# Block products for three quarters of an MLP down-projection, with weight sums on GpSimd

## The chip, the core and the metric

The kernel runs on one core of a Trainium2 chip. A core has five engines that run side by side, each through its own list of instructions in order: TensorE (PE; its weight loads are listed as PEld), VectorE (DVE), ScalarE (ACT), GpSimd (POOL) and SyncE (SP), which here only issues DMAs. They wait for each other by semaphores. The metric is the device time of one execution in microseconds (us); the median of several runs is compared.

## What is computed

The reference is one decoder block on 512 tokens of width 1024 in float32. Two token mixers (a state-space scan and a gated delta rule) are merged by gates and projected; then comes a squared-ReLU MLP. Each of the two parts has a norm ahead and one behind:

```python
x = x + g1 * rmsnorm(merged @ w_out, norm_mix_post)
h = rmsnorm(x, norm_mlp_pre) * (1.0 + sc2) + sh2
y = jnp.square(jax.nn.relu(h @ w_mlp_up)) @ w_mlp_down      # 1024 -> 4096 -> 1024
x = x + g2 * rmsnorm(y, norm_mlp_post)
```

The change concerns the last product, `... @ w_mlp_down`, and what stands between `merged @ w_out` and it.

## The kernel before

**Matmuls.** Every float32 operand is split into two float32r parts, hi and lo. ACT makes hi by a cast, DVE makes lo by subtracting hi from the raw value (`dense_w`, L140 to L147: `raw` by a DMA on SP, `sc.copy` at L145, `ve.tensor_sub` at L146). `mm3` (L149 to L152) then issues three matmuls for each pair of tiles: hi x hi, lo x hi, hi x lo. `raw`, `whi` and `wlo` have three buffers each.

**Order of work.** The first 870 us (projections in, scans) are ordered by a planner written into the kernel (`Weave`) and are not touched, apart from four small tables and `eye`, which the change allocates in another pool. Behind it, from the up-projection of the two mixers on, the order within each engine is made by the framework when the kernel is built: it goes through an estimate of time and places an instruction on its engine when its inputs and its buffers are free there, the one written earlier first. So an instruction can stand in its engine's list far ahead of its place in the program. On the chip each engine takes its list in that order. A pool's memory that is given to a later pool can be used only after the earlier pool's last reader.

**From the output projection to the MLP** (L1268 to L1356). The pool `yp` of the up-projection is closed (L1268), and `lp` is opened. The rows for the two gates are loaded (`adr`, then a bias row added and a norm row multiplied in on DVE, L1275 to L1279), as are the four residual tiles `x1` (L1284). The output projection goes by halves of the tokens (`half`) and halves of the columns (`hf`), with four weight tiles `kp` each (L1333 to L1348). `sums` squares on ACT; `norms(half)` (L1303 to L1325) takes the root on POOL (L1308), scales on DVE (L1313), adds the residual, one half of the columns on POOL and one on DVE (L1318), squares again on ACT (L1322), takes the second root on POOL (L1324) and scales into `xn` (L1325). `chans(half)` transposes `xn` on TensorE (L192) and makes the split `h2`. `up_part` computes the first three hidden tiles for one half of the tokens, so that TensorE has something to do while the second half is normed.

**The MLP** (L1359 to L1438) goes by quarters `q` of the 4096 hidden channels. In a quarter, eight hidden tiles (128 channels x 512 tokens, 24 matmuls of 128x512 each) are made, squared and split into `act` (L1375 to L1379). Then `down` (L1382) goes over two halves of the output columns `hf` and four weight tiles `kp`; in each, four token tiles x two channel tiles x three matmuls of 128x512. The four banks are copied to `ya` in the first quarter and added to it on DVE (L1410) in the others. The last quarter ends with the norm and the output.

PSUM has eight banks; `lpsum` hands them out in turn.

## Time and profile before

| | |
|---|---|
| median of 3 runs | 1483.22 us (1481.3 to 1486.84) |
| the profiled execution, its own time | 1484.77 us |
| its span (first to last instruction) | 1483.1 us, granted clock 0.996 |
| TensorE busy, weight loads busy | 1458.1 us (98%), 1241.0 us (84%) |
| DVE, ACT, POOL busy | 862.5 us (58%), 732.6 us (49%), 370.2 us (25%) |
| matmuls | 8592 |
| HBM | 181.1 MB read, 16.88 MB written, 133 GB/s over the span |

Busy matmuls overlap, since each record holds the passage through the array; the distance from one start to the next tells more than a record's length. In a table of stretches each engine has its busy time in the stretch and, in brackets, its number of instructions; then come the granted clock, the share of time in which the DMA engines were busy, and their rate. A group of instructions has its line, engine, operation and tiles, its count, its busy time and the mean of one in ns, and behind the bar the idle time of the engine ahead of it with what ended it.

### The profile page before, as it was taken

To read this page: it belongs to the slowest core of one execution; us is meant where nothing else is said; L and a number is where in the kernel's file an instruction comes from. 1 tells how busy PE (TensorE), PEld (TensorE's weight loads), DVE (VectorE), ACT (ScalarE), POOL (GpSimd) and SP (SyncE) were. 2 spreads that over 40 slices of the span, in tenths; PEclk is the share of its full clock that TensorE was granted. 3 is DMA by queue.
4 is the path that set the end of the run, shared out by engine and by line. 5 is a ranking of instruction groups with operands and counts; after the bars stand their busy time and mean duration, and the time that the engine had idled before them with its cause. 6 is when DMAs were issued, how large, how long until landed. Compare 5 with 4: busy or idle time off the path is not lost. (4 is left out here: it accounts for less than half of the span.)

```text
span 1483.1 us, 22692 instructions
## 1 busy us (share of the span) xinstructions
PE 1458.1 (98%) x8592; PEld 1241.0 (84%) x8592; DVE 862.5 (58%) x1522; ACT 732.6 (49%) x1379; POOL 370.2 (25%) x691
## 2 busy tenths in 40 slices
PE   9999999999999999999999899999999999999998
PEld 7788898879989889888888788888878888888886
DVE  3565577677767777676777634444477324343444
ACT  6575545673764747645665635333355333132232
POOL 3005444341814607336623410000011000000002
PEclk9999999999999999999999999999999999999999
DMA  9323434543434524344343449543372233223221
GB/s 360 127 97 118 150 103 125 128 137 97 151 119 138 158 81 151 121 116 138 116 137 119 158 170 331 175 156 127 110 239 88 97 100 100 89 96 99 93 95 69
DMA packets 87070, 199.47 MB, mean 134 GB/s; under 512 B 32504, under 2 KB 33024, under 8 KB 86960
## 3 DMA queue, kind: packets, MB, share of 16 engines
q1 hardware_dynamic: 86960, 198.01, 41.3%
q8 instruction: 68, 1.11, 0.3%
q14 instruction: 42, 0.34, 0.1%
HBM read 181.10 MB, written 16.88 MB: 133 GB/s over the span
## 5 line engine op out<-in xcount | busy, mean ns | idle before, releaser
L150 PE MATMUL ps<-hT,whi 128*128 128x512 f32 x688 | 285.7, 415 | 4.8 <-ACT whi L469 4.3
L151 PE MATMUL ps<-hT,wlo 128*128 128x512 f32 x688 | 269.8, 392 | 1.2 <-DVE wlo L471 1.2
L152 PE MATMUL ps<-hT,whi 128*128 128x512 f32 x688 | 269.9, 392 | 0.0
L146 DVE TENSOR_TENSOR wlo<-raw,whi 128x1024 fp32r<-128x1024 f32 x114 | 140.0, 1229 | 199.7 <-ACT whi L145 199.7
L145 ACT CAST whi<-raw 128x1024 fp32r<-128x1024 f32 x114 | 119.4, 1048 | 210.1 <-PE pl L151 61.9
L150 PE MATMUL ps<-whi,hT 128*128 128x256 f32 (+1 forms) x536 | 166.3, 310 | 2.2 <-ACT y L715 1.4
L471 DVE TENSOR_TENSOR wlo<-raw,whi 128x1024 fp32r<-128x1024 f32 x103 | 128.1, 1244 | 64.2 <-ACT whi L469 60.3
L150 PEld LDWEIGHTS ps<-hT,whi 128*128 128x128 f32 x688 | 129.9, 189 | 31.9 <-ACT whi L469 4.5
L152 PE MATMUL ps<-wlo,hT 128*128 128x256 f32 (+1 forms) x536 | 154.3, 288 | 0.6 <-DVE wlo L471 0.6
L151 PE MATMUL ps<-whi,hT 128*128 128x256 f32 (+1 forms) x536 | 153.8, 287 | 0.0
L152 PEld LDWEIGHTS ps<-hT,whi 128*128 128x128 f32 x688 | 129.7, 189 | 28.3
L151 PEld LDWEIGHTS ps<-hT,wlo 128*128 128x128 f32 x688 | 130.1, 189 | 25.8 <-DVE wlo L471 2.4
L469 ACT CAST whi<-raw 128x1024 fp32r<-128x1024 f32 x103 | 107.3, 1044 | 67.4 <-PE ps L152 47.1
L533 DVE SCALAR_TENSOR_TENSOR cv<-ps,col,cv 128x511 f32<-128x511 f32 (+1 forms) x180 | 133.0, 742 | 8.0 <-ACT cv L527 5.4
L150 PEld LDWEIGHTS ps<-whi,hT 128*128 128x128 f32 x536 | 102.1, 190 | 5.8 <-ACT y L715 1.6
L825 POOL TENSOR_TENSOR tm<-Ub,Nb 128x60 f32<-128x60 f32 (+24 forms) x248 | 93.7, 378 | 52.5 <-DMA Nb<-btd 37.6
L151 PEld LDWEIGHTS ps<-whi,hT 128*128 128x128 f32 x536 | 102.1, 190 | 2.2
L152 PEld LDWEIGHTS ps<-wlo,hT 128*128 128x128 f32 x536 | 101.8, 190 | 2.0 <-DVE wlo L471 0.8
L827 POOL TENSOR_TENSOR Ub<-Ub,tm 128x60 f32<-128x60 f32 (+24 forms) x248 | 95.0, 383 | 19.4
L1416 POOL TENSOR_TENSOR ya<-ya,gate 128x512 f32<-128x512 f32 x4 | 5.8, 1466 | 324.8 <-ACT junk L1414 324.8
L150 PE MATMUL pl<-hT,whi 128*128 128x512 f32 (+1 forms) x184 | 66.6, 363 | 1.0 <-DVE hT L195 1.0
L151 PE MATMUL pl<-hT,wlo 128*128 128x512 f32 (+1 forms) x184 | 66.1, 362 | 0.4 <-DVE wlo L146 0.4
(502 smaller groups left out, 3049.0 us busy)
## 6 DMA issues: line engine op xcount, KB each, us to landing
raw<-in_w_ch SPq DMA_DIRECT2D x81, 512.0 KB
raw<-in_w_ada SPq DMA_DIRECT2D x48, 512.0 KB
raw<-in_w_z SPq DMA_DIRECT2D x32, 512.0 KB
raw<-in_w_up SPq DMA_DIRECT2D x32, 512.0 KB
raw<-in_w_mu SPq DMA_DIRECT2D x32, 512.0 KB
raw<-in_w_md SPq DMA_DIRECT2D x32, 512.0 KB
dc<-acd SPq DMA_DIRECT2D x16, 512.0 KB
ydr<-y SPq DMA_DIRECT2D x32, 256.0 KB
```

Source lines behind the costliest of these rows:

```text
L145: sc.copy(hi, raw)
L146: ve.tensor_sub(out=lo, in0=raw, in1=hi.bitcast(F32))
L150: pe.matmul(ps, lhsT=lhs[0], rhs=rhs[0], start=first, stop=False)
L151: pe.matmul(ps, lhsT=lhs[1], rhs=rhs[0], start=False, stop=False)
L152: pe.matmul(ps, lhsT=lhs[0], rhs=rhs[1], start=False, stop=last)
L469: sc.copy(hi, raw)
L471: ve.tensor_sub(out=lo, in0=raw, in1=hi.bitcast(F32))
L533: ve.scalar_tensor_tensor(out=t[:, s:], in0=ps[:, :T - s], scalar=col[:, o + k:o + k + 1], in1=t[:, s:], op0=MUL, op1=ADD)
L825: gp.tensor_tensor(out=t3, in0=Ub[:, 0:r, j:j + 1].to_broadcast([P, r, n]), in1=Nb[:, j:j + 1, j + 1:32].to_broadcast([P, r, n]), op=MUL)
L827: gp.tensor_tensor(out=Ub[:, 0:r, j + 1:32], in0=Ub[:, 0:r, j + 1:32], in1=t3, op=SUB)
L1416: gp.tensor_tensor(out=y, in0=y, in1=gates[1][:, hs], op=MUL)
```

## The change

**Seven products instead of eight.** Two hidden tiles (k = 0, 1) and two halves of the tokens make four blocks of the squared activations, a0 to a3 (`a[:, 2k + half]`, 256 tokens each); two hidden tiles and two halves of the output columns make four blocks of weights (`b[hf][:, k]`). The plain product takes eight block products. The change uses a known form with seven, with sums of blocks as factors: on the activations a0, a2; the two sums in `s12`; a0 - a1 and a3; a2 less a sum; on the weights `b[0]`, the two sums in `t`, the two differences that are written back into `b`, and one more in `b[1][:, 1]`. It does so in the first three quarters (`down7`), in four stages of two, two, two and one product, each over four weight tiles `kp`, two token tiles and the three matmuls of a split product. Some products are added to two outputs: their bank is read, and matmuls go on adding to it in the next stage (`pa`, `pb_`). A quarter so has 14 additions to `ya`.

**Who does it.** The sums of weights and of activations are made on POOL. The splits are made on ACT and DVE as before, but from the sums, on the activations for each of the first three stages (`unit`), with the subtraction of the fourth on POOL; `ahead` makes those of stages three and four some steps early. The first quarter's weights are loaded by DMAs that POOL issues, and their sums made, beside the output projection's first half; the other quarters' are loaded by SP.

**What moves.** The rows of the gates and the residual tiles are loaded on POOL's queue from within the output projection (`residual`), into a pool that is open only until the MLP. So `x1` is stored to DRAM after each norm (`x1d`) and loaded again for the last quarter. The last quarter keeps its code.

```diff
-    tok1 = const.tile([P, NC, P], F32, name="tok1")
+    tok1 = sp.tile([P, NC, P], F32, name="tok1", bufs=1)
...
-    lp = ctx.enter_context(tc.tile_pool(name="lp", bufs=1))
-    gates = []
-    for n in range(2):
-        g = fin.tile([P, D], F32, name=f"gate{n}")
-        nc.sync.dma_start(out=g, in_=adr[n].partition_broadcast(P))
-        for r, fn in ((n, ve.tensor_add), (2 + n, ve.tensor_mul)):
-            bb = lp.tile([P, D], F32, tag="ob", name="rb", bufs=2)
-            nc.sync.dma_start(out=bb, in_=rows[r].partition_broadcast(P))
-            fn(out=g, in0=g, in1=bb)
-        gates.append(g)
+    x1d = dram.tile([NC, P, D], F32, name="x1d")
+    gate1 = fin.tile([P, D], F32, name="gate1")
+    rp = ctx.enter_context(tc.tile_pool(name="rp", bufs=1))
+
+    def quarter_weights(q, kp, en):
+        b = []
+        for hf in range(2):
+            b.append(rp.tile([P, 2, T], F32, tag="wr", name="wr", bufs=8))
+            en.dma_start(out=b[hf].rearrange("p a b -> p (a b)"), in_=w_md[q, hf, kp])
+        t = rp.tile([P, 2, T], F32, tag="tt", name="tt", bufs=4)
+        gp.tensor_tensor(out=t[:, 0], in0=b[1][:, 0], in1=b[0][:, 0], op=SUB)
+        gp.tensor_tensor(out=t[:, 1], in0=b[1][:, 1], in1=t[:, 0], op=SUB)
+        gp.tensor_tensor(out=b[1][:, 0], in0=b[1][:, 1], in1=b[1][:, 0], op=SUB)
+        return b[0], b[1], t
...
+    def residual():
+        for n, g in enumerate((gate0, gate1)):
+            gp.dma_start(out=g, in_=adr[n].partition_broadcast(P))
+            for r, fn in ((n, ve.tensor_add), (2 + n, ve.tensor_mul)):
+                bb = lp.tile([P, D], F32, tag="ob", name="rb", bufs=2)
+                gp.dma_start(out=bb, in_=rows[r].partition_broadcast(P))
+                fn(out=g, in0=g, in1=bb)
+        for t in range(NC):
+            xx = lp.tile([P, D], F32, name=f"x1{t}")
+            gp.dma_start(out=xx, in_=x[t * P:(t + 1) * P, :])
+            x1.append(xx)
...
+            nc.sync.dma_start(out=x1d[t], in_=x1[t])
...
                 if half and hf and kp == 2:
                     chans(0)
+                if not half and not hf and kp == 2:
+                    residual()
+                if not half and hf:
+                    first_q.append(quarter_weights(0, kp, gp))
...
+    def halves(src, dst, en):
+        sc.copy(dst[0], src)
+        en.tensor_tensor(out=dst[1], in0=src, in1=dst[0].bitcast(F32), op=SUB)
+        return dst
+
+    def unit(src, n, en):
+        u = mp.tile([P, 2, n, 256], F32R, tag="act", name="unit", bufs=8)
+        return halves(src, (u[:, 0], u[:, 1]), en)
+
+    def wide(src, en=None):
+        n = src.shape[1]
+        return halves(src, [wp.tile([P, 2, T], F32R, tag=tag, name=tag)[:, 0:n] for tag in ("whi", "wlo")], en or ve)
+
+    def product(ps, u, ub, w, wb, tt, first, last):
+        ts = slice(tt * P, (tt + 1) * P)
+        for n, (i, j) in enumerate(((0, 0), (1, 0), (0, 1))):
+            pe.matmul(ps, lhsT=u[i][:, ub, ts], rhs=w[j][:, wb], start=first and n == 0, stop=last and n == 2,
+                      skip_group_check=True)
+
+    def down7(q):
+        ab, pr, u1, u2 = [], [], [], []
+        for kp in range(4):
+            ab.append(first_q[kp] if q == 0 else quarter_weights(q, kp, nc.sync))
+            a = mp.tile([P, 4, 256], F32, tag="pr", name="pr", bufs=4)
+            for k in range(2):
+                _, rl = hidden(q * 8 + 2 * kp + k)
+                sc.activation(a[:, 2 * k:2 * k + 2].rearrange("p a b -> p (a b)"), rl, AF.Square)
+            pr.append(a)
+            sm = mp.tile([P, 2, 256], F32, tag="s12", name="s12", bufs=4)
+            gp.tensor_tensor(out=sm[:, 0], in0=a[:, 1], in1=a[:, 3], op=ADD)
+            gp.tensor_tensor(out=sm[:, 1], in0=sm[:, 0], in1=a[:, 0], op=SUB)
+            gp.tensor_tensor(out=a[:, 1], in0=a[:, 0], in1=a[:, 1], op=SUB)
+            u1.append(unit(a[:, 0:4:2], 2, ve))
+            gp.tensor_tensor(out=a[:, 2], in0=a[:, 2], in1=sm[:, 1], op=SUB)
+            if kp:
+                u2.append(unit(s12, 2, ve))
+            s12 = sm
+        u2.append(unit(s12, 2, ve))
...
+        def ahead():
+            n = step[0]
+            step[0] += 1
+            if 3 <= n < 7:
+                u3.append(unit(pr[n - 3][:, 1:4:2], 2, ve))
+            elif 7 <= n < 11:
+                u4.append(unit(pr[n - 7][:, 2:3], 1, gp))
+
+        def stage(us, ws, plan, read=None):
+            for kp in range(4):
+                ahead()
+                w = ws(kp)
+                for n, (ps, ub, wb, start) in enumerate(plan if kp < 3 else plan[::-1]):
+                    for tt in range(2):
+                        product(ps[tt], us[kp], ub, w, wb, tt, start and kp == 0, kp == 3)
+                        if kp == 3 and n == 0 and read:
+                            read(tt)
...
+        def w1(kp):
+            b1, _, t = ab[kp]
+            w = wide(b1)
+            gp.tensor_tensor(out=b1[:, 1], in0=b1[:, 1], in1=t[:, 1], op=SUB)
+            return w
+
+        def w3(kp):
+            w = [wp.tile([P, 2, T], F32R, tag=tag, name=tag) for tag in ("whi", "wlo")]
+            for n in range(2):
+                halves(ab[kp][n][:, 1 - n], (w[0][:, n], w[1][:, n]), ve)
+            return w
+        stage(u1, w1, [(pc, 1, 1, True), (pa, 0, 0, True)], lambda tt: add(tt, 0, pa[tt], True))
+        for tt in range(2):
+            add(tt, 0, pc[tt])
+        pb_ = banks()
+        stage(u2, lambda kp: wide(ab[kp][2]), [(pb_, 0, 0, True), (pa, 1, 1, False)],
+              lambda tt: add(tt, 1, pa[tt], True))
+        for tt in range(2):
+            add(tt + 2, 1, pb_[tt], True)
+        pc = banks()
+
+        def third(tt):
+            add(tt + 2, 1, pa[tt])
+            add(tt + 2, 0, pa[tt], True)
+        stage(u3, w3, [(pc, 1, 0, True), (pa, 0, 1, False)], third)
+        for tt in range(2):
+            add(tt + 2, 0, pc[tt])
+        stage(u4, lambda kp: wide(ab[kp][1][:, 1:2]), [(pb_, 0, 0, False)])
+        for tt in range(2):
+            add(tt, 1, pb_[tt])
+
+    for q in range(3):
+        down7(q)
...
+    x1 = [rp.tile([P, D], F32, tag="tt", name="x1r", bufs=4) for _ in range(NC)]
+    for t in range(NC):
+        nc.sync.dma_start(out=x1[t], in_=x1d[t])
```

`add` copies a bank to `ya` on ACT (the first time in quarter 0) or adds it there on DVE.

More of the change, by code (lines that the diff above doesn't have):

```diff
@@ L401, in hybrid_block @@
     H = 48
-    tok1 = const.tile([P, NC, P], F32, name="tok1")
-    tok2 = const.tile([P, NC, P], F32, name="tok2")
-    neg = const.tile([P, NC, 16], F32, name="neg")
-    elast = const.tile([P, H, NC], F32, name="elast")
+    tok1 = sp.tile([P, NC, P], F32, name="tok1", bufs=1)
+    tok2 = sp.tile([P, NC, P], F32, name="tok2", bufs=1)
+    neg = sp.tile([P, NC, 16], F32, name="neg", bufs=1)
+    elast = sp.tile([P, H, NC], F32, name="elast", bufs=1)
     nA = const.tile([H, 1], F32, name="nA")
@@ L415, in hybrid_block @@
         gp.memset(tl, 0.0)
-    eye = const.tile([P, 8, 32], F32, name="eye")
+    eye = sp.tile([P, 8, 32], F32, name="eye", bufs=1)
     gp.memset(eye, 0.0)
@@ L1268, in hybrid_block @@
     up.close()
-    lp = ctx.enter_context(tc.tile_pool(name="lp", bufs=1))
-    gates = []
-    for n in range(2):
-        g = fin.tile([P, D], F32, name=f"gate{n}")
-        nc.sync.dma_start(out=g, in_=adr[n].partition_broadcast(P))
-        for r, fn in ((n, ve.tensor_add), (2 + n, ve.tensor_mul)):
-            bb = lp.tile([P, D], F32, tag="ob", name="rb", bufs=2)
-            nc.sync.dma_start(out=bb, in_=rows[r].partition_broadcast(P))
-            fn(out=g, in0=g, in1=bb)
-        gates.append(g)
-    x1, xn = [], []
-    for t in range(NC):
-        xx = fin.tile([P, D], F32, name=f"x1{t}")
-        nc.sync.dma_start(out=xx, in_=x[t * P:(t + 1) * P, :])
-        x1.append(xx)
+    x1d = dram.tile([NC, P, D], F32, name="x1d")
[11 more added lines that the diff above has]
+        return b[0], b[1], t
+    norm_scope = ExitStack()
+    lp = norm_scope.enter_context(tc.tile_pool(name="lp", bufs=1))
+    gate0 = lp.tile([P, D], F32, name="gate0")
+    x1, xn = [], []
+    def residual():
[9 more added lines that the diff above has]
+            x1.append(xx)
     h2 = [(chan_tile(), chan_tile()) for _ in range(KD)]
@@ L1309, in norms @@
         for t in tt:
-            xx = lp.tile([P, D], F32, tag="act", name="xn", bufs=16)
+            xx = lp.tile([P, D], F32, tag="xn", name="xn", bufs=4)
             for i in range(2):
@@ L1330, in chans @@
             to_channels(lp, lpsum, None, 1, xn, (h2[kt][0][:, cs], h2[kt][1][:, cs]), kt, (2 * half, 2 * half + 1))
-    pp = {}
+    pp, first_q = {}, []
     for half in range(2):
@@ new lines, in hybrid_block, with hidden @@
+    norm_scope.close()
+    mp = ctx.enter_context(tc.tile_pool(name="mp", bufs=1))
+    ya = [mp.tile([P, D], F32, name=f"ya{t}") for t in range(NC)]
+    sq = [mp.tile([P, 1], F32, name=f"sqn{t}") for t in range(NC)]
+    def hidden(mm):
+        if mm < len(ups):
+            ps = ups[mm][1]
+        else:
+            w = dense_w(w_mu[mm])
+            ps = lpsum()
+            for k in range(KD):
+                ks = slice(k * P, (k + 1) * P)
+                mm3(ps, (w[0][:, ks], w[1][:, ks]), h2[k], k == 0, k == KD - 1)
+        rl = mp.tile([P, T], F32, tag="rl", name="rl", bufs=2)
+        sc.activation(rl, ps, AF.Relu)
+        return ps, rl
@@ new lines, in down7, with add @@
+    def down7(q):
[17 more added lines that the diff above has]
+        u2.append(unit(s12, 2, ve))
+        def add(tt, hf, ps, first=False):
+            y = ya[tt][:, hf * T:(hf + 1) * T]
+            if first and q == 0:
+                sc.copy(y, ps)
+            else:
+                ve.tensor_add(out=y, in0=ps, in1=y)
+        u3, u4, step = [], [], [0]
+        def ahead():
[14 more added lines that the diff above has]
+                            read(tt)
+        banks = lambda: [lpsum() for _ in range(2)]
+        pa, pc = banks(), banks()
+        def w1(kp):
[26 more added lines that the diff above has]
+            add(tt, 1, pb_[tt])
@@ new lines, in hybrid_block, with down @@
+    for q in range(3):
+        down7(q)
+    act = []
+    for m in range(8):
+        ps, rl = hidden(24 + m)
+        a = mp.tile([P, 2, T], F32R, tag="act", name="act", bufs=8)
+        s = mp.tile([P, T], F32, tag="pr", name="sq", bufs=4)
+        ve.scalar_tensor_tensor(out=s, in0=ps, scalar=0.0, in1=rl, op0=MAX, op1=MUL)
+        sc.activation(a[:, 0, :], rl, AF.Square)
+        ve.tensor_sub(out=a[:, 1, :], in0=s, in1=a[:, 0, :].bitcast(F32))
+        act.append(a)
+    def down(ps, t, w, kp, a=0, b=T):
+        ts = slice(t * P, (t + 1) * P)
+        for k in range(2):
+            kk = 2 * kp + k
+            mm3(ps[:, a:b], (act[kk][:, 0, ts], act[kk][:, 1, ts]),
+                (w[0][:, k * T + a:k * T + b], w[1][:, k * T + a:k * T + b]), kk == 0, kk == 7)
```

120 lines of the change are left out of this document (43 added, 77 removed).

## The prediction

> **What bounds the kernel now.** I read the page first, then the stretches of the last 410 us, then single rows.
>
> ```profile
> span 1483.1 us, 22692 instructions
> PE 1458.1 (98%) x8592; PEld 1241.0 (84%) x8592; DVE 862.5 (58%) x1522; ACT 732.6 (49%) x1379; POOL 370.2 (25%) x691
> ...
> PEclk9999999999999999999999999999999999999999
> ...
> PE 40%; DVE 2%; DMA 1%; issue 0%; ACT 0%; POOL 0%; POOLq 0%; SPq 0%; DVEq 0%; ACTq 0%
> ```
>
> TensorE is busy 98% of the span at full granted clock, and the chain of waits hardly names anything else, so the time is the number of matmuls times their spacing, plus the few places where TensorE starves.
>
> The table of stretches, one line each (us, then busy time and instruction count by engine, clock, DMA share, GB/s):
>
> ```profile
> 1074.00:1094.00 20.00, 20.00 (x90) 16.53 (x89) 13.45 (x13) 10.15 (x16) 0.00 (x0) 1.00 0.82 277
> 1094.00:1116.00 22.00, 20.45 (x97) 16.34 (x96) 16.87 (x26) 13.01 (x22) 5.72 (x5) 1.00 0.63 203
> 1116.00:1134.00 18.00, 15.61 (x117) 13.86 (x116) 14.72 (x37) 9.23 (x18) 5.91 (x5) 1.00 0.10 33
> 1211.00:1255.00 44.00, 44.00 (x196) 36.40 (x195) 18.86 (x22) 16.14 (x24) 0.00 (x0) 1.00 0.30 96
> 1255.00:1299.00 44.00, 44.00 (x191) 35.69 (x190) 15.76 (x17) 9.25 (x10) 0.00 (x0) 1.00 0.29 96
> ```
>
> The last two are one MLP quarter: up (22 DVE instructions) and down (17). TensorE has no gap, DVE and ACT are under half busy and POOL, where the change puts much of its work, does nothing. The first three are output projection and norms; there TensorE loses 1.55 + 2.39 us, and the DMA share reaches 0.82.
>
> **What is removed: 72 matmuls.** A down quarter issues 2 halves x 4 weight tiles x 4 token tiles x 2 x 3 = 192 matmuls of 128x512. Its spacing comes from where the phases begin:
>
> ```profile
> 1211.11 0.39 PE L150 MATMUL pl<-hT,whi 128*128 128x512 f32 x1
> ...
> 1254.64 0.40 PE L150 MATMUL pl<-whi,act 128*128 128x512 f32 x1
> ...
> 1299.27 0.39 PE L150 MATMUL pl<-hT,whi 128*128 128x512 f32 x1
> ```
>
> Up takes 43.53 us / 192 = 0.2267 us each, down 44.63 / 192 = 0.2324. A quarter by block products has 7 products of 4 tiles x 2 token tiles x 3 = 168 matmuls of the same shape. Three quarters save 72 x 0.2324 = **16.7 us**. If the products ran at the spacing of up, it would be 3 x (44.63 - 168 x 0.2267) = 19.6 us; the stationary operand stays an activation slice as in down, so I take 16.7.
>
> **What is added on ACT and DVE, per quarter.**
>
> ```profile
> L146 DVE TENSOR_TENSOR wlo<-raw,whi 128x1024 fp32r<-128x1024 f32 x80 | 98.3, 1231 | 118.1 <-ACT whi L145 118.1
> L145 ACT CAST whi<-raw 128x1024 fp32r<-128x1024 f32 x80 | 83.7, 1046 | 138.8 <-PE pl L151 61.9 <-PE ps L151 49.9 <-PE ps L152 15.7
> L1379 DVE TENSOR_TENSOR act<-sq,act 128x512 fp32r<-128x512 f32 x32 | 21.9, 685 | 0.0
> L1378 ACT ACTIVATE act<-rl 128x512 fp32r<-128x512 f32 x32 | 20.1, 629 | 0.0
> L1410 DVE TENSOR_TENSOR ya<-pl,ya 128x512 f32<-128x512 f32 x14 | 9.5, 688 | 3.1 <-PE pl L152 2.8
> ```
>
> DVE after: 16 splits of 1024 columns (8 up, 8 in the first two stages) x 1.23 = 19.7; 24 splits of 512 (12 activation sums, 8 weights of stage three, 4 of stage four) x 0.685 = 16.4; 14 additions instead of 8 x 0.688 = 9.6: 45.7 us where the two windows show 34.6. ACT: 16 x 1.05, 24 casts and 8 squares at 0.63, 8 Relu of much the same: about 43 us. A quarter on TensorE becomes 43.5 + 39.0 = 82.5 us, so both have room on average.
>
> The narrow place is the product stages: 39.0 us of TensorE against 9.8 + 5.5 + 2.7 (weights) + 2.7 (third stage's activation sums) + 9.6 (additions) = 30.3 us of DVE. Weights have three buffers, so a split may start two steps (2 x 2.79 us) ahead. At the seams a bank is read and written again: the bank closes 6 matmuls before the stage ends and is next used after 6 more, 12 x 0.2324 = 2.8 us; two additions of 0.69 need 1.4 plus latency. That is hidden unless DVE is more than about 1.2 us behind. The last stage has steps of 1.39 us, and in its 5.6 us DVE has six additions, two splits and the next up split, 4.1 + 1.4 + 1.2 = 6.7 us, some 1 us over. No row shows such a seam: at best 0, at worst 1 us at each of 3 seams in 3 quarters, 9. I take 0.8 us a quarter, **+2.5**, nearer to nothing because this kernel's own bank seams (L1410) show no matmul waiting for them.
>
> **What is added on POOL.** Each quarter 16 subtractions of 512 columns and 20 operations of 256. Their nearest rows (shortest/median/longest ns):
>
> ```profile
> L1416 POOL TENSOR_TENSOR ya<-ya,gate x4: 1289/1380/1812, 1451.4 to 1456.8; 128x512 f32<-128x512 f32 x4
> ...
> L1156 POOL TENSOR_TENSOR xk<-xk,zs x32: 733/744/1721, 228.1 to 870.7; 128x256 f32<-128x256 f32 x32
> ...
> L471 DVE TENSOR_TENSOR wlo<-raw,whi x103: 1209/1226/1759, 56.1 to 857.8; 128x1024 fp32r<-128x1024 f32 x103
> ```
>
> 16 x 1.29 + 20 x 0.74 = 35.4 us alone, of 82.5. Per up pair (10.9 us) it is 3 x 1.29 + 4 x 0.74 = 6.8 us, so POOL keeps up, and what it makes is needed a stage later (11 us). But both engines now and then take most of another's instruction longer: 744 becomes 1721, 1226 becomes 1759. That is one waiting out the other.
>
> The Trainium skill, "SBUF — State Buffer", section "Who interferes with whom", says why: a DVE instruction with two SBUF inputs and a GpSimd instruction that reads SBUF share a port, and the second blocks until the first is done. This trace agrees (1721 against 744 ns). By the rule nearly all splits here contend with the new POOL work; it is the slower rival below.
>
> **What is moved.** Now SP loads gate and residual rows early, and only the bias and norm rows late:
>
> ```profile
> 911.39 0.90 SPq L1275 DMA_DIRECT2D gate<-adr  x2
> ...
> 914.73 1.35 SPq L1284 DMA_DIRECT2D x<-in_x  x2
> ...
> 1073.88 0.80 SPq L1278 DMA_DIRECT2D rb<-in_rows  x2
> ```
>
> ```profile
> 1073.12 0.69 DVE L1266 TENSOR_TENSOR hT<-ma,hT 128x512 fp32r<-128x512 f32 x1
> ```
>
> L1278 goes out 0.07 us after the last reader of the up-projection's pool. Gate 0 and the residual move into that later space, so with the first quarter's weights 17 of 18 DMAs of 512 KB now start there, all on POOL's queue, gate 1's `adr` row alone being free earlier. Bandwidth: 277 GB/s at share 0.82 makes about 340 GB/s when full (estimate). From 1074 to 1116 the rows above carry 20 x 277 + 22 x 203 = 10.0 MB, of which 2 MB are the rows; 18 x 0.52 = 9.4 MB plus two stores of x1 make 18.4 MB, 54 us at 340. So the loads run to about 1128, the weights last. For the issue, SP takes 0.4 us each (0.80 for 2); POOL's nearest is one operation, 1.29: 7 to 23 us for 18, ending at 1081 to 1097, and the residual's ten of them by 1087 at the latest, ahead of the first use of gate 0 (1094.91, below).
>
> The Trainium skill, "DMA: Bandwidth & Descriptors", section "Latency and other measured facts", puts the first byte of a GpSimd-issued DMA at about 1 us, spent on emitting it; as an estimate that is 18 us for 18, between the bounds. No run here shows it yet.
>
> What stands behind them on POOL is the norm chain:
>
> ```profile
> 1116.92 0.70 POOL L1308 TENSOR_TENSOR r<-r,mhalf 128x2 f32<-128x2 f32 x1 [13.38 <-DVE r L1307]
> 1118.48 2.96 POOL L1318 TENSOR_TENSOR x<-xn,x 128x512 f32<-128x512 f32 x2 [0.86 <-DVE xn L1313]
> 1124.13 1.73 POOL L1324 TENSOR_TENSOR s<-s,mhalf 128x1 f32<-128x1 f32 x1 [2.69 <-DVE s L1323]
> 1126.86 0.55 POOL L1324 TENSOR_TENSOR s<-s,mhalf 128x1 f32<-128x1 f32 x1 [1.00 <-DVE s L1323]
> ```
>
> ```profile
> 1094.91 2.07 DVE L1313 SCALAR_TENSOR_TENSOR xn<-pl,r,gate 128x512 f32<-128x512 f32 x3 [1.04 <-POOL r L1308]
> ...
> 1127.44 0.75 DVE L1325 TENSOR_SCALAR xn<-x,s 128x1024 f32<-128x1024 f32 x1 [0.73 <-POOL s L1324]
> ```
>
> ```profile
> 1128.26 0.60 PE L192 MATMUL pl<-ident,xn 128*128 128x128 f32 x4
> ```
>
> The second half's `xn` is ready at 1128.19 (the last root ends at 1127.41, L1325 follows), and TensorE starts on it 0.07 us later. So delay of a POOL step there goes to the end one for one. Three times in turn (root, residual addition, root) the chain comes back to POOL, which may then be in a weight sum: nothing if the sums are done by 1117, all twelve (12 x 1.47 = 17.6) if they stand ahead. Against it, the removal of SP's rows from among the weight loads may give back the one long wait there, 1.2 us on L146. By the bandwidth the sums of the last one or two weight tiles come after 1117, so I take one sum of 1.3 at each of three returns: **+4** (from -1 to +18). SP also gets four stores of x1, which wait for that chain with the next up weights behind them; three raw buffers cover some 3 x 5.4 us.
>
> Past the three quarters nothing changes on the path: the last one and the output are as before, and reloading x1 (four DMAs) lies under the last quarter's 192 up matmuls. The small tables that change pools change address only.
>
> **Sum.** -16.7 + 2.5 + 4 = -10.2. Span 1483.1 becomes 1472.9; the profiled execution lasted 1484.77, 1.67 around its span, so 1474.6 for one like it. It was 1.55 above the median of 1483.22, which makes the forecast **1473.0**.
>
> **Rivals.** (1) All cover holds: seams and norms cost nothing, 1483.2 - 16.7 = 1466.5. For it speaks that DVE and ACT are half idle; against it that TensorE waits already at the second norm.
> (2) POOL's queue holds the norms: ten or more sums or loads ahead of the root of the second half, +14 to 17.6 with 2.5 of seams: about 1484, no change. For it speaks the 54 us of loads into 42; against it that the sums come in pairs of tiles as they land, with room for the root between.
> (3) Slower: the port. In the stages DVE has 39.0 - 30.3 = 8.7 us free. POOL has 4 x 1.29 + 4 x 0.74 = 8.1 there, and the next quarter's 12 sums (15.5) if they come early. If DVE waits out all, 53.9 us in 39.0: 14.9 lost in each of two quarters (the third has no next sums), 1483.2 - 16.7 + 29.8 + 4 = 1500. It decides once more than 8.7 us of a quarter's stages is lost to POOL. Against it: the sums need buffers which the fourth stage frees, so they fall into the up phase.
> (4) The products do not run at the spacing assumed, since the last stage's 1.39 us steps wait for splits: 0.5 us x 12 steps more, 1479.
>
> **Chances.** Forecast 0.54 (its own range 1468 to 1478), (1) 0.18, (2) 0.17, (3) 0.07, (4) 0.04. A measurement can tell 0.5%, 7.4 us: below 1475.8 is faster, above 1490.6 slower. Faster: (1) and four fifths of the forecast, 0.61; slower: (3), 0.07; the rest, 0.32. The range leaves out half of (1), at the low end, the dear end of (2), and (3): 1466 to 1484.
>
> **What would show it.** TensorE with 8520 matmuls; quarters of 82 to 84 us instead of 88.2 (1211.11 to 1299.27); in them no wait over 1 us at a split or an addition; POOL with some 106 to 125 us more; the stretch from the last output-projection matmul to the first full up matmul longer by 1 to 7 us with a POOL root or sum behind it. Wrong would be: gaps inside the stages of several us (then 3 or 4), or an unchanged norm stage (then 1).

## The result and the profile after

The changed kernel is slower: 1495.34 us, median of 4 runs (1494.33 to 1497.62), against 1484.08 us for 4 runs of the kernel before; ratio 1.0078, 95% interval 1.0055 to 1.0101. The forecast was 1473.0 us, faster. The page of the profile after, its span, its engines, the clock and the queue that POOL issues:

```profile
span 1493.2 us, 22889 instructions
...
PE 1447.0 (97%) x8520; PEld 1228.5 (82%) x8520; DVE 929.9 (62%) x1570; ACT 777.2 (52%) x1463; POOL 517.5 (35%) x817
...
PEclk9999999999999999999999999999997999999999
...
q0 software_dynamic: 2592, 9.44, 1.8%
```

The 72 matmuls are gone and TensorE's busy time fell by 11.1 us, yet the span grew by 10.1. The stretches of the norm stage and of the second quarter (hidden tiles, then products), in the columns used before:

```profile
1074.00:1094.00 20.00, 17.23 (x75) 13.54 (x74) 9.54 (x8) 7.17 (x12) 6.78 (x13) 1.00 0.93 329
1094.00:1116.00 22.00, 19.04 (x82) 14.78 (x81) 13.20 (x10) 7.90 (x9) 13.23 (x11) 1.00 0.94 348
1116.00:1134.00 18.00, 3.78 (x17) 2.63 (x16) 9.56 (x13) 5.38 (x11) 12.18 (x11) 0.67 0.48 170
1134.00:1150.00 16.00, 14.88 (x94) 13.03 (x94) 12.14 (x29) 7.96 (x18) 4.91 (x5) 0.84 0.34 133
...
1227.21:1270.79 43.58, 43.58 (x193) 36.02 (x192) 20.12 (x17) 18.40 (x27) 22.71 (x19) 1.00 0.32 104
1270.79:1311.95 41.16, 39.79 (x169) 31.34 (x168) 38.21 (x40) 21.40 (x34) 23.39 (x18) 1.00 0.28 89
```

From 1116 to 1134 TensorE has 17 instructions where it had 117. The DMA share is 0.93 and 0.94 in the two stretches ahead, where it was 0.82 and 0.63. In the quarter, DVE is busy 38.21 of 41.16 us of the products; the forecast had counted 30.3 of 39.0.

Set out by stages, each from the start of its first matmul to the start of the next stage's, in us. "Norm stage" runs from the first output-projection matmul to the first product (down matmul before) of the first quarter, "last" from the first hidden tile of the last quarter to the end:

| kernel | norm stage | products 1 | hidden 2 | products 2 | hidden 3 | products 3 | last | span |
|---|---|---|---|---|---|---|---|---|
| before | 98.31 | 44.64 | 43.53 | 44.63 | 43.54 | 44.63 | 95.6 | 1483.1 |
| after | 119.36 | 40.19 | 43.58 | 41.16 | 43.89 | 41.09 | 96.3 | 1493.2 |

The norm stage lost 21.05 us. The three quarters gained 4.45 + 3.42 + 3.19 = 11.06, and the last stage lost 0.7.

Where the 21 us appear, by the timelines of the kernel after. TensorE:

```profile
1093.13 0.50 PE L152 MATMUL pl<-wlo,hT 128*128 128x512 f32 x1 [2.45 <-DVE wlo L146]
...
1132.45 1.09 PE L192 MATMUL pl<-ident,xn 128*128 128x128 f32 x4 [13.87 <-issue]
```

DVE, the step ahead of the first half's root:

```profile
1098.82 0.17 DVE L1324 TENSOR_SCALAR r<-r 128x2 f32<-128x2 f32 x1
```

POOL, on which that root (L1325) stands:

```profile
1102.16 1.48 POOL L1282 TENSOR_TENSOR tt<-wr 128x512 f32<-128x512 f32 x1 [10.71 <-DMA wr<-in_w_md]
...
1117.45 1.29 POOL L1284 TENSOR_TENSOR wr<-wr 128x512 f32<-128x512 f32 x1
1118.69 0.71 POOL L1325 TENSOR_TENSOR r<-r,mhalf 128x2 f32<-128x2 f32 x1
1121.80 1.42 POOL L1282 TENSOR_TENSOR tt<-wr 128x512 f32<-128x512 f32 x1 [2.40 <-DMA wr<-in_w_md]
...
1127.06 2.50 POOL L1335 TENSOR_TENSOR x<-xn,x 128x512 f32<-128x512 f32 x2
```

The root's input is ready at 1098.99; the root runs at 1118.69, behind nine weight sums and the waits for their loads (POOL stood still for 10.71 us waiting for the first). Three more sums stand between the root and the residual addition (L1335). TensorE waits 13.87 us ahead of the transposes of the first half; the profile names no releaser there ("issue"), but the transposes read `xn`, which that chain makes.

### The profile page after: what moved, and what is told of

It reads as the page before. It is cut to its first block, busy times and chain, and to the rows that moved or that the text cites. A ratio compares the mean times of both kernels' runs of the same rounds, so it can differ in the third digit from the quotient of the medians.

```text
span 1493.2 us, 22889 instructions
## 1 busy us (share of the span) xinstructions
PE 1447.0 (97%) x8520; PEld 1228.5 (82%) x8520; DVE 929.9 (62%) x1570; ACT 777.2 (52%) x1463; POOL 517.5 (35%) x817
## 5 line engine op out<-in xcount | busy, mean ns | idle before, releaser
L146 DVE TENSOR_TENSOR wlo<-raw,whi 128x1024 fp32r<-128x1024 f32 x90 | 119.4, 1328 | 152.9 <-ACT whi L145 152.8
L471 DVE TENSOR_TENSOR wlo<-raw,whi 128x1024 fp32r<-128x1024 f32 x103 | 128.9, 1253 | 63.1 <-ACT whi L469 61.7
L145 ACT CAST whi<-raw 128x1024 fp32r<-128x1024 f32 x90 | 94.3, 1048 | 127.8 <-PE pl L152 42.3
L469 ACT CAST whi<-raw 128x1024 fp32r<-128x1024 f32 x103 | 107.3, 1044 | 69.2 <-PE ps L152 48.5
L1418 PE MATMUL pl<-whi,unit 128*128 128x512 f32 x240 | 75.5, 396 | 1.0 <-DVE ya L1448 1.0
L1402 DVE TENSOR_TENSOR wlo<-wr,whi 128x512 fp32r<-128x512 f32 (+1 forms) x48 | 51.2, 1090 | 38.3 <-ACT whi L1401 33.9
```

The lines of the kernel that those rows point to most:

```text
L145: sc.copy(hi, raw)
L146: ve.tensor_sub(out=lo, in0=raw, in1=hi.bitcast(F32))
L469: sc.copy(hi, raw)
L471: ve.tensor_sub(out=lo, in0=raw, in1=hi.bitcast(F32))
L1402: en.tensor_tensor(out=dst[1], in0=src, in1=dst[0].bitcast(F32), op=SUB)
L1418: pe.matmul(ps, lhsT=u[i][:, ub, ts], rhs=w[j][:, wb], start=first and n == 0, stop=last and n == 2, skip_group_check=True)
```

## The experiments

Stages in all of them are read as above; the numbers are gathered in one table at the end. The first six split the norm stage and the last five the quarters. Where the text gives no ratio, the kernel ran once, and its stages and span are those of that one execution.

**Without the first quarter's sums.** Only the 12 sums go; the loads stay where they are. The first quarter then multiplies unsummed weights.

```diff
-                    first_q.append(quarter_weights(0, kp, gp))
+                    first_q.append(quarter_weights(0, kp, gp, False))   # loads, no sums
```

> The changed kernel with the 12 sums of the first quarter's weights on POOL left out (the first quarter then uses unsummed weights; all 18 loads stay on POOL's queue). In the changed kernel the first half's root L1325 runs at 1118.7, 20 us after its input, and TensorE idles 13.9 us. Theory A (POOL's list: the root stands behind sums that wait for their loads): the root runs within 2 us of its input, the idle stretch of 13.9 us shrinks to under 3 us, span 1476 to 1481. Rival B (DMA bandwidth: 18 loads make the gate, the residual and the output projection's weights late): the idle stretch stays above 8 us and the span above 1486.

The wait ahead of the transposes fell to 1.4 us (from 13.87), and the norm stage to 108.24 us: 11.1 us of the 21 are the sums. The span, 1483.3 us, was above the 1476 to 1481 expected, since 9.9 us of the norm stage remained.

**The sums moved, nothing left out.** The loads stay on POOL's queue; the 12 sums are placed behind the second half's last `hT` (the tiles that `chans` makes from the transposed `xn`).

```diff
+    mark = gp.tensor_tensor(out=flag, in0=lo, in1=lo, op=ADD)      # lo: last column of the last hT
+    with tc.issue_after(mark.ins):
+        first_q = [quarter_sums(b) for b in first_q]
```

> The changed kernel with one thing moved and nothing left out: the first quarter's 12 weight sums stand on POOL behind the last hT of the second half (by a 128x1 operation that reads that tile), instead of beside the output projection. All loads stay where the change has them, on POOL's queue. Theory A (the place of the sums on POOL's list alone made 11 of the 21 us of the norm stage; the rest is the early loads and the rows): the first half's root runs within 1 us of its input, TensorE's wait ahead of the transposes falls from 13.9 to under 2 us, norm stage 106 to 109 us, first quarter's products 40 to 42, span 1480 to 1485. Rival B (the loads keep POOL or DVE as late as the sums did): wait over 8 us, norm stage over 114.

The norm stage took 108.22 us, as without the sums (108.24), the wait ahead of the transposes was 1.58 us, and the first products took 41.73. The root ran at 1098.15 with its input ready at 1097.83. So it is the place on POOL's list that cost 11 us, not the work. The span was 1485.7, just over the range expected.

**First quarter's weights late.** Their loads and sums go where those of the other quarters are; the rows and the residual stay on POOL's queue.

```diff
-                    first_q.append(quarter_weights(0, kp, gp))
...
-            ab.append(first_q[kp] if q == 0 else quarter_weights(q, kp, nc.sync))
+            ab.append(quarter_weights(q, kp, nc.sync))
```

> The changed kernel with the first quarter treated as the second and third: its weights loaded on SP and summed within the quarter, the pool for them opened behind the norms. The ten row and residual loads stay on POOL's queue. Both theories: norm stage shorter. A: the root runs within 2 us of its input, the time from the start of the output projection to the first product falls from 119.4 us to 103 to 107 (99 before the change gave 98.3), the first quarter's products take about 41 us like the other two; span 1477 to 1482, ratio to before 0.995 to 1.0. B: the same stretch 100 us, since only ten of 18 loads are left.

Norm stage 105.22, as expected, but products 46.40 in place of 41: ratio 1.0041 (1.0025 to 1.0057), where faster was expected. So 3.0 us more of the norm stage belong to the early loads, and 7.1 us above the 98.1 of the kernel that undoes both remain. DVE's timeline of this kernel shows them:

```profile
1082.26 1.23 DVE L1297 TENSOR_TENSOR gate<-gate,rb 128x1024 f32<-128x1024 f32 x1 [3.90 <-DMA rb<-in_rows]
1083.41 1.22 DVE L146 TENSOR_TENSOR wlo<-raw,whi 128x1024 fp32r<-128x1024 f32 x1
...
1090.72 1.23 DVE L1297 TENSOR_TENSOR gate<-gate,rb 128x1024 f32<-128x1024 f32 x1 [3.54 <-DMA rb<-in_rows]
1091.86 1.22 DVE L146 TENSOR_TENSOR wlo<-raw,whi 128x1024 fp32r<-128x1024 f32 x1
...
1095.30 1.22 DVE L1297 TENSOR_TENSOR gate<-gate,rb 128x1024 f32<-128x1024 f32 x1 [2.23 <-DMA rb<-in_rows]
```

and TensorE's what follows from it:

```profile
1093.13 0.50 PE L152 MATMUL pl<-wlo,hT 128*128 128x512 f32 x1 [2.70 <-DVE wlo L146]
1097.72 0.50 PE L152 MATMUL pl<-wlo,hT 128*128 128x512 f32 x1 [1.57 <-DVE wlo L146]
1104.88 0.50 PE L152 MATMUL pl<-wlo,hT 128*128 128x512 f32 x1 [1.43 <-DVE wlo L146]
```

The gate's operations wait on DVE for their rows, and the splits of the output projection's weights stand behind them. TensorE loses 5.7 us to it. The first of these operations ran at 1082.26; in the kernel before it ran at 1078.85. POOL's list adds to the lateness:

```profile
1083.79 0.54 POOL L1296 DMA_DIRECT2D rb<-in_rows  x1 [7.51 <-DVE gate L1297]
1084.32 0.54 POOL L1300 DMA_DIRECT2D x<-in_x  x1
1086.06 0.54 POOL L1296 DMA_DIRECT2D rb<-in_rows  x1 [1.21 <-DVE gate L1297]
```

`rb` has two buffers. The third row's load therefore waits on POOL for the first gate operation, and the loads listed behind it wait too.

**Rows and residual early.** The residual and the gates' first rows are loaded on SP into a pool opened ahead of the up-projection's, the bias and norm rows late on SP as in the kernel before; the first quarter's loads and sums stay on POOL.

```diff
+    xp = xs.enter_context(tc.tile_pool(name="xp", bufs=1))
...
-            gp.dma_start(out=g, in_=adr[n].partition_broadcast(P))
+            nc.sync.dma_start(out=g, in_=adr[n].partition_broadcast(P))
```

> The changed kernel with gate 0 and the residual in a pool opened ahead of the up-projection, so that SP loads them early as before the change; the first quarter's eight weight loads and 12 sums stay on POOL beside the output projection. A: the root still stands behind all 12 sums; with eight loads instead of 18 these are done some 8 to 10 us earlier, so the idle stretch of 13.9 us falls to 3 to 7 us, span 1482 to 1487. B: with the bandwidth relieved the norm stage is as before the change, idle under 2 us, span 1472 to 1476.

Neither came: norm stage 115.63, span 1491.5. All twelve sums now stood ahead of the first root, and TensorE lost 3.93 and 8.85 us to splits of the weights instead of 13.87 ahead of the transposes. The 8.85 us are the old cause in a new place and under a new name: on DVE's list `xn`, which waits for the root, stands ahead of the split. The 3.93 us, at 1094.51, come before the root and are another matter: DVE waits for a row, and its operations beside POOL's sums take twice their length.

```profile
1089.56 2.70 DVE L1300 TENSOR_TENSOR gate<-gate,rb 128x1024 f32<-128x1024 f32 x1 [2.73 <-DMA rb<-in_rows]
1092.18 2.28 DVE L146 TENSOR_TENSOR wlo<-raw,whi 128x1024 fp32r<-128x1024 f32 x1
```

**Both undone.** The seven products are kept; rows early, the first quarter's weights late.

> Both moves undone: rows and residual early on SP, first quarter's weights on SP within the quarter. What is left is the three quarters by block products with the sums of their weights and activations on POOL. Both theories: norm stage as before the change (98 to 100 us from the start of the output projection to the first product), three quarters of 84.5 to 86 us instead of 88.2; span 1472 to 1476, ratio to before 0.992 to 0.996. If the span stays above 1480, the loss is not in the two moves.

The norm stage is that of the kernel before, 98.11 us. But the products of the first quarter took 46.54, and the ratio was 0.9989 (0.9975 to 1.0002), no difference that can be told: the other two quarters still gain, and the first has lost its own. Three of its eight hidden tiles are made beside the norms, which leaves POOL less time ahead of the products than in the other quarters; the last group of activation sums started 8.3 us after the first product, and TensorE waited 3.49 and 1.40 us.

**Early loads, sums behind the norms.** Rows early; the loads on SP, half of them behind the first half's up-projection; the sums behind the last root of the second half.

```diff
+    with tc.issue_after(last.ins):          # last: second half's last root on POOL
+        first_q = [quarter_weights(0, kp, raw[kp]) for kp in range(2)]
...
```

> The changed kernel with its norm stage repaired and its first quarter's weights still early: the two gates' rows and the residual are loaded on SP ahead of the up-projection, as in the kernel before; the first quarter's eight loads go on SP, half of them ahead of the second half's norms and half behind the first half's up-projection; and the 12 weight sums are placed by an explicit order behind the last root of the second half on POOL. Theory A (the norm stage loses its 21 us to the sums and the waits for their loads ahead of the roots, to the late rows and to the early loads, and to nothing else): norm stage 98 to 101.5 us, products of the first quarter 40 to 41.5, whole span 1473 to 1477, so 0.4 to 0.8 per cent faster than before. Rival B (two quarters' worth of loads and sums cannot be had for nothing: POOL's 12 sums of 1.3 to 1.7 us, now at 1126 to 1145, lock DVE's xn and hT work or come too late for the first quarter's products): norm stage over 103 or products over 44, span 1480 or more.

The rival was right: 1.0028 (1.0009 to 1.0046), norm stage 112.83. DVE, grouped for 1129.5 to 1146 in this kernel, while POOL made sums:

```profile
L195 DVE CAST hT<-hf 128x256 fp32r<-128x256 f32 x6 | 8.0, 1358 | 1.1 <-ACT hf L194 1.1
L196 DVE TENSOR_TENSOR hT<-hf,hT 128x256 fp32r<-128x256 f32 x5 | 6.0, 1225 | 0.1
```

and for 1126 to 1135 in the kernel with both undone, where POOL was idle:

```profile
L196 DVE TENSOR_TENSOR hT<-hf,hT 128x256 fp32r<-128x256 f32 x8 | 3.2, 422 | 0.1
L195 DVE CAST hT<-hf 128x256 fp32r<-128x256 f32 x8 | 2.2, 289 | 2.0 <-ACT hf L194 2.0
```

The same cast takes 1358 ns instead of 289: each of these long DVE operations ends 0.1 to 0.3 us after a POOL operation of 1.3 to 1.5 us has ended, as if it had waited for it. Here this stands on the path, since TensorE waits for `hT`. The row of the stretches adds that the clock fell to half:

```profile
1134.00:1150.00 16.00, 11.71 (x42) 9.38 (x43) 13.72 (x15) 3.10 (x6) 11.67 (x9) 0.50 0.00 1
```

**No sums on POOL at all, and no weight sums.** Two kernels on the base of the last one; their products use unsummed blocks.

> The same kernel with all sums of weights and of activations on POOL left out in all three quarters (the products then use unsummed blocks, the output is not the reference's); only u4's four subtractions a quarter and the norms' own work stay on POOL. Matmuls, splits, loads and adds are as before. In the changed kernel each quarter's products took 41.1 to 41.2 us in the second and third quarters against 39.0 by their count of 168 x 0.2324. Theory A (the 2 us a quarter are lost because DVE's splits are stretched while POOL runs, unit from some 0.69 to 1.2 us): the group of 128x512 units falls under 0.85 us on average and the products to 39.3 to 40.2. Rival B (the stages lose it by their chains: ACT copy, DVE subtraction, three adds out of PSUM, whatever POOL does): units fall too, but the products stay at 40.8 to 41.3.

> Only the weight sums left out (16 operations of 128x512 a quarter; the output is not the reference's), the activation sums stay on POOL. If DVE is held by POOL's work as such, products lie between those with all sums and those with none, by the share of POOL's time: some 25 of 40 us a quarter go, so about two thirds of whatever the kernel without any sums gains. If the wait of the products is for the activation sums themselves (u1, u2 late at the quarter's first products), nothing is gained here and all of it without them.

Without any sums the products took 39.03, 39.03 and 39.04 us, which is their count, 168 x 0.2324 = 39.04: the chains at the seams by themselves cost nothing. Without the weight sums alone they took 39.09, 39.21 and 39.08, not the two thirds expected but all of the gain. The norm stage of this second kernel, 97.65 us with the same early loads as in the kernel with the sums behind the norms (112.83), shows that there the sums cost the 15 us, and not the loads. DVE's groups (from the first product to the last quarter) show that this is not a matter of how much DVE is stretched. After, 1187 to 1397:

```profile
L1402 DVE TENSOR_TENSOR wlo<-wr,whi 128x512 fp32r<-128x512 f32 x36 | 33.5, 960 | 8.7 <-ACT whi L1401 4.2 <-PE pl L1418 4.0
...
L1402 DVE TENSOR_TENSOR unit<-pr,unit 128x512 fp32r<-128x512 f32 x21 | 25.8, 1236 | 0.0
L1448 DVE TENSOR_TENSOR ya<-pl,ya 128x512 f32<-128x512 f32 x29 | 18.4, 679 | 0.0
...
L1402 DVE TENSOR_TENSOR unit<-s,unit 128x512 fp32r<-128x512 f32 x10 | 11.6, 1160 | 0.4
```

Without weight sums, 1163 to 1376:

```profile
L1408 DVE TENSOR_TENSOR wlo<-wr,whi 128x512 fp32r<-128x512 f32 x36 | 27.8, 797 | 17.0 <-ACT whi L1407 13.4 <-PE pl L1424 3.1
...
L1408 DVE TENSOR_TENSOR unit<-pr,unit 128x512 fp32r<-128x512 f32 x21 | 20.3, 974 | 0.0
...
L1408 DVE TENSOR_TENSOR unit<-s,unit 128x512 fp32r<-128x512 f32 x10 | 11.6, 1159 | 0.4
```

The units from `s12` are as slow as after the change (1159 ns) and cost nothing. That leaves which DVE work is held, and when, as what matters; the next three kernels try it. The additions out of PSUM, `ya`, were never held (679 ns).

**All sums, in the hidden stages.** Rows early and loads on SP as above; in each quarter the 12 sums stand behind the groups of activation sums.

```diff
+            with tc.issue_after(last.ins):      # last: last activation sum of this kp
+                for k in ((0, 1), (2,), (3,), ())[kp]:
+                    ab.append(quarter_sums(raw[k]))
```

> The same sums as in the changed kernel, none left out, but all of them at places where DVE has little to do: gates' rows and residual early on SP, the first quarter's loads on SP (half ahead of the second half's norms, half behind the first half's up-projection), and in each quarter the 12 weight sums are pinned on POOL behind the groups of activation sums of the same quarter's hidden stage (6 behind the first group, 3 behind the second, 3 behind the third), where the trace of the kernel without weight sums shows POOL idle for some 7 us between groups. Theory A (the sums cost only because each of DVE's operations beside them waits for a POOL operation of 1.3 us to end, in the norm stage and in the last stage of the products, and because they stand ahead of the roots): norm stage 97.5 to 100 us, products 39.1 to 40.0 in each quarter, span 1463 to 1469, ratio 0.986 to 0.990. Rival B (the sums' work is the price wherever it stands, POOL being the bound of a quarter once it holds 12 + 4 weight sums and 16 activation sums): second-stage products wait for the sums of the last tiles, products 42 or more, span 1474 or more.

The norm stage is whole (97.48 us), but the products took 46.53, 42.81 and 43.53; ratio 0.9995 (0.9985 to 1.0005). These are rival B's times. Of its reason one part shows, that the second stage's products wait for what POOL makes last: the last group of activation sums comes late. That the work is the price wherever it stands is not shown by this, and the two kernels below speak against it. In the second quarter, whose first product is at 1255.81, POOL's rows

```profile
1258.02 2.28 POOL L1485 TENSOR_TENSOR wr<-wr,tt 128x512 f32<-128x512 f32 x1
1260.26 1.19 POOL L1439 TENSOR_TENSOR s<-pr 128x256 f32<-128x256 f32 x1
```

lead to ACT's, and the two to TensorE's:

```profile
1262.62 0.62 ACT L1406 CAST unit<-s 128x512 fp32r<-128x512 f32 x1 [3.38 <-POOL s L1440]
```

```profile
1267.42 0.50 PE L1423 MATMUL pl<-wlo,unit 128*128 128x512 f32 x1 [1.92 <-DVE wlo L1407]
```

**The last group first.** Six of the first quarter's sums start with the last `hT`; in each quarter the four updates (`b1 - t1`, L1476 of the kernel after) stand behind the last group.

> The kernel with spread sums, with two changes of POOL's order and none of its work (but one 128x1 operation): the first quarter's first 6 weight sums start behind the last hT of the second half (at about 1133 instead of 1143, by a 128x1 operation on POOL that reads that tile), its other 6 behind the first and second group of activation sums; and in each quarter the four updates of the first half's weights stand behind the last group of activation sums instead of ahead of it. In the kernel with spread sums the last group started 8.3 us (first quarter) and 4.5 us (second) after the first product, where the kernel without weight sums had it some 2.5 us after it, and PE lost 4.9 and 2.8 us about 9 to 12 us into the products. Theory A (what the quarters lose now is that this last group, and with it the last unit, ACT's next casts and the first split of the second stage, comes late on POOL's list): the last group starts 2.3 to 3.0 us after the first product, PE's wait there is under 0.7 us, products 39.1 to 40.0 in each quarter, norm stage 97.5 to 99.5, span 1463 to 1469, ratio 0.986 to 0.990. Rival B (DVE is what is late: its splits beside POOL's work take 1.2 to 1.8 us instead of 0.7 to 1.2, wherever the last group stands): products stay at 41 or more, span 1473 or more.

Products 40.92, 42.63 and 42.64, norm stage 98.17; ratio 0.9943 (0.9930 to 0.9957), faster than the kernel before, at half of what was expected. The last group started 2.3 us after the first product, as theory A had it, and the first quarter gained 5.6 us; the second gained 0.2 and the third 0.9. There the four updates now stood in a row beside the second stage, 2.0 us long on average instead of 1.3, and TensorE waited three times in each (the second quarter's):

```profile
1262.55 0.50 PE L1429 MATMUL pl<-wlo,unit 128*128 128x512 f32 x1 [0.86 <-DVE wlo L1413]
...
1267.07 0.74 PE L1429 MATMUL pl<-whi,unit 128*128 128x512 f32 x2 [0.54 <-DVE ya L1465]
1269.28 0.73 PE L1429 MATMUL pl<-whi,unit 128*128 128x512 f32 x2 [1.24 <-DVE ya L1465]
```

**The updates apart.** They get a tile of their own (`ud`; `s12` goes from four buffers to two for the space), and in the second and third quarter they and the first six sums start with the hidden stage.

```diff
+        u = rp.tile([P, T], F32, tag="ud", name="ud", bufs=4)
+        gp.tensor_tensor(out=u, in0=b[0][:, 1], in1=t[:, 1], op=SUB)
...
+            mark = gp.tensor_tensor(out=flag, in0=done, in1=done, op=ADD)   # done: last add of the quarter before
+            with tc.issue_after(mark.ins):
+                ab += [quarter_sums(raw[k]) for k in range(2)]
```

> The kernel with the marks, and one more step: the four updates of the first half's weights (b1 - t1) go to a tile of their own, so that in the second and third quarter they need not wait for the first stage's reading and no longer stand beside the second stage; they, and the sums of the first two tiles, start with the hidden stage (behind the last add of the quarter before), where POOL was idle for 28 us. The first quarter keeps its order. In the kernel with the marks each of these four operations took 2.0 us at 1259.7 to 1267.5, and PE lost 0.86, 0.54 and 1.24 us to DVE's splits and adds beside them, of 3.6 us by which the second and third quarters' products (42.6) exceed their count (39.0). Theory A (POOL's operations beside the second stage are what the products still lose to): products of the second and third quarter 39.2 to 40.3, first quarter 40.9 as it was, span 1471 to 1474 where the stages ahead take as long, ratio 0.989 to 0.992. Rival B (the second stage's chain of four adds out of PSUM and its splits is too long for DVE by itself): products of the two quarters 41.8 or more, ratio 0.993 to 0.996 as before.

Products 40.94, 39.11 and 39.21, 1469.97 us (1467.23 to 1471.94), ratio 0.9903 (0.9886 to 0.9921): faster than both kernels. Theory A held, with the second quarter and the span slightly better than it said. Its page and the stretches of its second quarter:

```profile
span 1470.2 us, 22875 instructions
```

```profile
1209.07:1252.63 43.56, 43.56 (x194) 36.05 (x192) 20.49 (x16) 18.39 (x27) 37.59 (x29) 1.00 0.39 127
1252.63:1291.74 39.11, 39.11 (x170) 31.58 (x169) 32.51 (x41) 21.41 (x34) 10.57 (x8) 1.00 0.21 72
```

Beside the kernel after, POOL has 37.59 us of work in the hidden stage instead of 22.71 and 10.57 in the products instead of 23.39. DVE's products stage falls from 38.21 to 32.51, and TensorE has no gap in it.

All stages together (those left out of a row differ by less than 1.2 us from the rows above):

| kernel | norm stage | products 1 | products 2 | products 3 | span |
|---|---|---|---|---|---|
| without the first sums | 108.24 | 39.95 | 41.84 | 41.08 | 1483.3 |
| the sums moved alone | 108.22 | 41.73 | 43.05 | 41.16 | 1485.7 |
| first weights late | 105.22 | 46.40 | 41.53 | 41.16 | 1486.4 |
| rows early | 115.63 | 40.21 | 42.15 | 41.09 | 1491.5 |
| both undone | 98.11 | 46.54 | 43.08 | 41.07 | 1480.2 |
| sums behind the norms | 112.83 | 40.19 | 43.12 | 41.08 | 1490.7 |
| no sums on POOL | 100.30 | 39.03 | 39.03 | 39.04 | 1467.4 |
| no weight sums | 97.65 | 39.09 | 39.21 | 39.08 | 1462.6 |
| sums in hidden stages | 97.48 | 46.53 | 42.81 | 43.53 | 1481.3 |
| last group first | 98.17 | 40.92 | 42.63 | 42.64 | 1477.2 |
| updates apart | 98.21 | 40.94 | 39.11 | 39.21 | 1470.2 |

The output projection itself began anywhere from 1064.85 to 1070.03 us in these profiles, though no edit changes the matmuls ahead of it (some open a pool or place loads there). Why is left open; it is the reason to compare stages and not spans.

## Why the prediction was wrong

**What is removed: right.** 8520 matmuls, and a quarter's products at 39.03 us where POOL makes no sums: the 16.7 us are there to be had.

**What failed most: the term "+4" of the moved part.** Its range was -1 to +18 us, and the norm stage lost 21.05. The term read "one sum of 1.3 at each of three returns", since "the sums come in pairs of tiles as they land, with room for the root between". The order on POOL's list is made when the kernel is built, and it put nine of twelve sums, with their waits for loads, ahead of the first half's root. On an engine that takes its list in order, a sum whose weights have not landed holds whatever stands behind it. The prediction priced the sums by their length, 1.3 us, and the wait ahead of them at nothing; the root came 19.7 us after its input. It also looked at the second half's root, whose result TensorE takes up 0.07 us later, and gave the first half's no price. Moving the sums gave back 11.1 us, as much as leaving them out.

**The rows: the step "by 1087 at the latest, ahead of the first use of gate 0 (1094.91)" asked the wrong question.** It priced an issue by its length alone, and an issue did take only 0.54 us. But POOL stood 8.01 us ahead of the third row's issue and 1.71 ahead of the fourth's, until a buffer was free, so that the last residual's issue ended at 1088.4. The rows landed later as well, against a DMA share of 0.93, and what stood behind them was not `xn` at 1094.91 but, from 1082, the splits of the output projection's own weights on DVE's list. The forecast had thought that moving the rows might give back 1.2 us of waiting at these splits. With the early loads it is 3.0 + 7.1 us; how much of it is the late landing and how much POOL's wait for buffers, no run separates. In this order of undoing, 11.1 + 3.0 + 7.1 = 21.2 of the 21.05 lost; in another order the parts would differ, as the kernel with early rows alone shows.

**The seams: "+2.5", 0.8 us a quarter, mis-sized and for another reason.** Measured against 39.04 it was 1.15 + 2.12 + 2.05 = 5.3 us. The chain of additions, which the term was about, costs nothing by itself. The count of 30.3 us for DVE took undisturbed lengths; with POOL beside it, DVE was busy 38.2. That is the mechanism of rival 3, which was given 14.9 us a quarter because it was taken to hold back every DVE operation. Its limit of 8.7 us of slack was not even used up (38.2 - 30.3 = 7.9), and still 2.1 us were lost: a few operations were late at the moment when TensorE needed them. Its counter-argument, that the sums fall into the up phase, was half right: POOL was busy 23.39 us in the products, 22.71 in the hidden stage. The activation sums hold DVE's units from `s12` just as long and cost 0.2 us at most in the kernel without weight sums.

**The first quarter's early sums were worth something.** With late weights its products took 46.4 to 46.5 us instead of 40.2. With early loads and sums in the hidden stage they took 46.53 as well, and with half of the sums started by the last `hT` 40.92. So it is the sums that have to be early, but they must not stand beside the norms.

**Rivals.** Rival 2 had the right kind of event, POOL's list holding the norms, with ten or more operations ahead of a root, at the wrong half and at 14 to 17.6 us; the waits for loads and the rows brought 21. At "no change" it was still too low: 1495.34 lies 11 us above the range. Rival 1's cover held neither in the quarters nor at the norms. Rival 4, late splits in the last stage's short steps, doesn't show: without sums on POOL the products took their count. The stages past the quarters cost 0.7 us, close to the nothing assumed. The signs that were named were the right ones: quarters of 84.74 and 84.98 us instead of 82 to 84, a norm stage longer by 21 instead of 1 to 7, with sums and a root of POOL behind it, and POOL busy 147 us more (517.5 against 370.2) instead of 106 to 125. POOL's operations too had been priced at their undisturbed lengths.

## What to carry to other kernels

Before work is given to an idle engine, list what else stands on that engine's list and on the critical path, and price a new operation at the wait for its inputs plus its length, for everything behind it; a DMA that lands late costs as much there as a long instruction. Two engines that hold each other make the idle time of one a poor measure of what it can take on: place the work in the stretch where the other's operations are not awaited, not where its data first arrive. Here the same seven products cost 11 us (1495.34 against 1484.08) or gained 13 (1469.97 against 1483.12), by the place of their sums and loads.

## What the runs showed of the hardware

**DVE beside POOL.** Casts of 128x256 took 289 ns alone (both undone) and 1358 while POOL subtracted 128x512 tiles (sums behind the norms), subtractions with both inputs in SBUF 422 and 1225. Additions with one input in PSUM took 679 ns in the changed kernel, and 688 in the kernel before, where POOL was idle. The Trainium skill, "SBUF — State Buffer", section "Who interferes with whom", says that a DVE instruction with at most one SBUF input outside the two-port modes does not contend, that one with two does, and that a cast can enter a two-port mode. These runs agree on the first two, and their casts were held. They add the size: a held operation of 128x256 takes about as long as one POOL operation, 1.2 to 1.4 us, which for the cast is more than four times its own length.

**The clock.** In the stretch that holds the wait of 13.87 us the granted clock was 0.67, and in the next 0.84. TensorE worked again from 1132.45; its matmuls of 128x256 came 0.21 us apart up to 1139.1, and 0.12 after:

```profile
1138.63 0.41 PE L150 MATMUL pl<-hT,whi 128*128 128x256 f32 x1
1138.85 0.41 PE L151 MATMUL pl<-hT,wlo 128*128 128x256 f32 x1
...
1139.23 0.28 PE L150 MATMUL pl<-hT,whi 128*128 128x256 f32 x1
1139.35 0.28 PE L152 MATMUL pl<-hT,whi 128*128 128x256 f32 x1
```

In the kernel with the sums behind the norms TensorE was busy 11.71 of 16 us, waiting again and again for `hT`, and the clock was 0.50. A wait so costs more than its length: here 6.7 us of work at half the rate followed it. The Trainium skill, "TensorE: Matmul & The Clock Gate", section "What's actually happening", has half rate after at least one idle window of about 3.4 us and full rate after at least one as long busy one. The trace agrees as far as it goes: the wait was longer than such a window, and so was the return, 6.7 us.

**DMAs issued by POOL** took 0.54 to 0.58 us each on POOL's list, for 512 KB each; where the tile's buffer was not yet free, POOL stood until it was, 8.01 us the longest time in the changed kernel.
